# Constants of a recurrent unit computed ahead, and two norms of a token block emitted whole at one stage boundary

## The chip, the cores and the metric

One Trainium2 chip, one core. The metric is the device time of one execution in microseconds (us). TensorE multiplies matrices, VectorE, ScalarE and GpSimd (DVE, ACT and POOL in the rows) work elementwise, and SyncE (SP) issues most DMAs.

## The reference, cut to what matters

512 tokens of width 1024 go through two blocks of a first kind (token mixer, convolutional FFN, each with a residual and a LayerNorm) and then two of a second kind. The first block of the second kind opens with an RMS norm and a gated recurrent unit. The change touches the boundary between the two kinds, and the constants of the recurrent unit:

```python
# end of the last block of the first kind
ffn = conv_ffn(x, ffn_w_up[l], ffn_conv_w[l], ffn_conv_b[l], ffn_w_down[l])
x = layer_norm(ALPHA * x + ffn, ln2_g[l], ln2_b[l])
...
# start of the second kind
hn = rms_norm_2(x, g[0])
proj = x @ w_in + b_in                        # x is hn here
...
log_a = -LRU_C * r_gate * jax.nn.softplus(-lam.astype(jnp.float32))
a = jnp.exp(log_a)
mult = jnp.sqrt(-jnp.expm1(2.0 * log_a))
```

`lam` is a vector of 1024 values that is known at the start. Its softplus does not depend on the tokens.

## The kernel before

Everything is fp32. Each product of two matrices is made of three matmuls of rounded high and low parts (`mm3`, L323 to L325): high by high, low by high, high by low. So the tokens are kept transposed as two tiles, `xTh` (written by ScalarE, L329) and `xTl` (written by VectorE, L331). Weights come in by DMA from SyncE's queue, are rounded on ScalarE (L285) and get their low part on GpSimd (L286).

The 512 tokens are four blocks of 128 rows; `x[:, t, :]` is block t. In the second FFN (`ffn` with `pre` set) the last part of the down projection runs block by block. When a block's second half has arrived (L897), `evac` starts a generator for it, `fin_row(t)`. Its first two parts are the LayerNorm `ln_fin`: mean and variance (L465, L467, L469), two halves centred and scaled by ScalarE and GpSimd (L472, L473), an inverse root by three Newton rounds of one-column VectorE rows (`rs1`, L411 to L417), then the scaling pair (L479; in block 3 also L477). The rest is the RMS norm `pre_norm`: squares with a sum on ScalarE (L944), the product with the gain into `work`, one half on GpSimd and one on VectorE (L960), another inverse root (L949 and `rs1`), and then a diagonal matrix `dg` with the root on it (L964). TensorE multiplies `work` by `dg` (L969), which scales and transposes at once, four 128x128 tiles into each of two banks named `tr`; L329 and L331 take each bank out to `xTh` and `xTl`.

`skew` keeps the open generators in a list. A call with a new generator moves every open one by one part, so consecutive blocks are in different parts; a call without one runs all that are open to their end.

The next stage is `rglru`. It first computes constants from `lam` (`sm8` and `lru` tiles, L1222 to L1242, twenty VectorE rows and one Exp on ScalarE, L1224), then calls `lead`: for its first two weight units it multiplies tokens 0 to 255 and then 256 to 511, 48 matmuls of 128x256 for each half, so that work can begin when two blocks are transposed. Later matmuls are 128x512.

A scheduler with a simulated timeline sets the order of each engine's rows within the dependences, so the order on an engine is not that of the code. A few rows are pinned by hand (`late`, `in_turn`). The activations that need another function table get an `ACT_TABLE_LOAD` in front of them.

Of the kernel before, what the change touches and what calls it, by code (L numbers as in the profile page):

```python
# [197 lines left out]
class Core:  # L198
# [656 lines left out]
    def ffn(self, l, x, xT, pre=None):  # L855

        nc = self.nc
        groups = [range(0, 8), range(8, 16), range(16, 22)]
        hs = {}

        def up(j):
            acc = []
            for o in (0, NF):
                ps = self.tmm(f"wu{l}", o + j, xT)
                a = self.t([128, 512], "tmp", 5, name="fup")
                nc.scalar.activation(a, ps, AF.Identity, scale=self.v(f"fc{l}2", o + j), bias=self.v(f"fb{l}", o + j))  # L866
                for d, tap in ((1, 1), (2, 0)):
                    nc.vector.scalar_tensor_tensor(a[:, d:], ps[:, :512 - d], self.v(f"fc{l}{tap}", o + j), a[:, d:],  # L868
                                                   op0=OP.mult, op1=OP.add)
                acc.append(a)  # L870
            nc.scalar.activation(acc[0], acc[0], AF.Gelu)
            nc.vector.tensor_mul(acc[0], acc[0], acc[1])
            tag = ("q", "k", "pt")[j % 3]
            nb = 9 if tag == "pt" else 8
            hh, hl = self.t([128, S], tag, nb, F32R, "hh"), self.t([128, S], tag, nb, F32R, "hl")
            self.split(hh, hl, acc[0])
            hs[j] = (hh, hl)

        g, b = self.row(4 * l + 2), self.row(4 * l + 3)
        xT2 = self.newT()  # L880
        st = {}
        if pre is not None:
            work = self.workset()

        def down(gi):
            js = list(groups[gi])
            fin = gi == 2
            for cb in range(2):
                nu = len(js) // 2
                u0 = cb * 11 + js[0] // 2  # L890

                def evac(t, ps, cb=cb):
                    s = slice(cb * 512, cb * 512 + 512)
                    if gi == 0:
                        nc.vector.scalar_tensor_tensor(x[:, t, s], x[:, t, s], ALPHA, ps, op0=OP.mult, op1=OP.add)
                    else:
                        nc.vector.tensor_add(x[:, t, s], x[:, t, s], ps)  # L897
                    if fin:
                        self.ln_half(x, t, cb, st)
                        if cb == 1:  # L900
                            self.skew(fin_row(t))
                if fin and cb == 1:
                    self.tokens([hs[j] for j in js], kept, evac)
                    continue
                kept = []

                def keep(i):
                    kept.extend(self.W_in(f"wn{l}", 11 + js[0] // 2 + i, *self.halves(KEEP["ffn"][i])))
                self.nmm(f"wn{l}", u0, [hs[j] for j in js], evac, nk=len(js),
                         side=[lambda i=i: keep(i) for i in range(nu)] if fin else ())  # L910
            if fin:
                self.skew()

        def fin_row(t):
            yield from self.ln_fin(x, t, st, g, b, None if pre is not None else xT2)
            if pre is not None:
                yield from self.pre_norm(x, t, pre, work[t], xT2)

        self.lead(f"wu{l}", LEADS["ffn"], xT)
        for j in range(10):  # L920
            up(j)
        down(0)
        for j in range(10, 18):
            up(j)
        down(1)
        for j in range(18, 22):
            up(j)
        down(2)
        return x, self.pairs(xT2)

# [280 lines left out]
            done = min(g[-1] + 3, 32)  # L1211
            down(gi)

    def rglru(self, x, xT):
        nc = self.nc

        lam = self.v("lam")
        z = self.t([128, 8], "sm8", 8)
        s = self.t([128, 8], "sm8", 8)
        s2 = self.t([128, 8], "sm8", 8)  # L1220
        p = self.t([128, 8], "sm8", 8)
        nc.vector.tensor_scalar(z, lam, -1.0, None, op0=OP.mult)  # L1222
        nc.vector.tensor_max(s, z, lam)
        nc.scalar.activation(s, s, AF.Exp, scale=-1.0)  # L1224
# [7 lines left out]
            nc.vector.scalar_tensor_tensor(p, p, 1.0 / c, s2, op0=OP.add, op1=OP.mult)  # L1232
        nc.vector.scalar_tensor_tensor(p, p, 1.0, s, op0=OP.add, op1=OP.mult)
        nc.vector.tensor_scalar(z, z, 0.0, None, op0=OP.max)
        sp = self.t([128, 8], "lru", 4)
        nc.vector.scalar_tensor_tensor(sp, p, 2.0, z, op0=OP.mult, op1=OP.add)
        m4 = self.t([128, 8], "lru", 4)
        p2 = self.t([128, 8], "lru", 4)
        nc.vector.tensor_scalar(m4, sp, -4.0, None, op0=OP.mult)
        nc.vector.tensor_scalar(p2, sp, 2.0, None, op0=OP.mult)  # L1240
        hb = self.t([128, 16], "lru", 4)
        nc.vector.tensor_scalar(hb, self.v("gb"), 0.5, None, op0=OP.mult)  # L1242
        yT = self.newT()
        self.lead("wli", LEADS["lru"], xT)
        tmp = lambda nm: self.t([128, 512], "tmp", 5, name=nm)
# [629 lines left out]
```

## Time and profile before

| | us |
|---|---|
| runs shown | 3902.67, 3887.15, 3885.52 |
| median | 3887.15 |
| profiled execution, own time | 3890.53 |
| its span on the core | 3888.4 |
| TensorE busy in it | 3684.4 (95%) |
| VectorE, ScalarE, GpSimd busy | 1725.2, 1488.5, 1602.0 |
| mean granted clock of TensorE | 0.969 of full speed |

The span is the time from the core's first to its last recorded instruction; the execution's own time lies 2.1 us above it. Every time in the rows below is counted from the start of that span. A granted clock of 1.00 is the level of 2.4 GHz, 0.50 that of 1.2 GHz.

### The profile page before, as it was taken

Reading aid. Unit: us, or ns where it says so; the run is one execution under the profiler, and the core shown is the slowest. Engines: PE = TensorE matmul, PEld = TensorE weight load, DVE = VectorE, ACT = ScalarE, POOL = GpSimd, SP = SyncE. Lnnn points to the kernel's source line nnn. Section 1 sums busy time; section 2 is a strip of 40 time slices with the busy share of each in tenths; the row PEclk is TensorE's granted clock in tenths of the full one; section 3 lists DMA queues with packets and bytes.
Section 4 is the critical chain, followed back from the end, with each engine's and each line's share of the span. In section 5 each row is a group of like instructions: output and inputs, shape, how many; then the busy total and the mean of one; then the engine's idle time right before and its main releaser. Section 6 shows DMA issues by size and latency. Waiting matters only on the chain.

```text
span 3888.4 us, 54978 instructions
## 1 busy us (share of the span) xinstructions
PE 3684.4 (95%) x21788; PEld 2976.9 (77%) x21788; DVE 1725.2 (44%) x3581; ACT 1488.5 (38%) x2669; POOL 1602.0 (41%) x831
## 2 busy tenths in 40 slices
PE   9999999999999999999998889999898878799998
PEld 8766777888897677778886777888766767688887
DVE  4553254533545424545336754322466564534123
ACT  4433333433344323334333644332364333343322
POOL 4422436444453223444444564344533111443444
PEclk9999999999999999999998999999999868899999
DMA  5311213223342122233331322233323312332332
GB/s 191 117 55 49 89 60 126 92 97 98 111 160 85 55 65 75 79 114 98 98 98 60 103 92 93 82 92 98 109 68 94 75 32 51 125 103 65 95 96 87
DMA packets 158386, 352.96 MB, mean 91 GB/s; under 512 B 63712, under 2 KB 71424, under 8 KB 157872
## 3 DMA queue, kind: packets, MB, share of 16 engines
q1 hardware_dynamic: 157856, 348.61, 28.8%
q8 instruction: 171, 2.80, 0.3%
q0 software_dynamic: 272, 0.84, 0.1%
q14 instruction: 87, 0.71, 0.1%
HBM read 331.53 MB, written 17.86 MB: 90 GB/s over the span
## 4 chain that ended last, share of the span: by engine, by line
PE 77%; DVE 9%; DMA 5%; POOL 4%; ACT 3%; issue 3%; SPq 0%; POOLq 0%; DVEq 0%; ACTq 0%
PE mm L323 13%; PE mm L325 13%; PE mm L324 13%; PE mm L385 6%; PE mm L384 5%; PE mm L386 5%; POOL wlo L286 2%; PE av L384 2%; PE av L386 2%; PE av L385 2%; PE sc L824 2%; PE mm L1687 2%; PE av L653 1%; PE tr L844 1%; ACT whi L285 1%
## 5 line engine op out<-in xcount | busy, mean ns | idle before, releaser
L286 POOL TENSOR_TENSOR wlo<-wst,whi 128x1024 fp32r<-128x1024 f32 (+2 forms) x524 | 1259.1, 2405 | 1789.3 <-PE mm L325 903.6
L285 ACT ACTIVATE whi<-wst 128x1024 fp32r<-128x1024 f32 (+2 forms) x524 | 548.9, 1047 | 1100.3 <-DMA wst<-in_wu 153.1
L323 PE MATMUL mm<-xTh,whi 128*128 128x512 f32 (+1 forms) x2208 | 832.1, 379 | 13.3 <-ACT whi L285 10.3
L324 PE MATMUL mm<-xTl,whi 128*128 128x512 f32 (+1 forms) x2208 | 833.9, 378 | 0.6
L325 PE MATMUL mm<-xTh,wlo 128*128 128x512 f32 (+1 forms) x2208 | 831.7, 378 | 0.0
L323 PEld LDWEIGHTS mm<-xTh,whi 128*128 128x128 f32 x2208 | 415.8, 189 | 100.3 <-ACT whi L285 12.2
L325 PEld LDWEIGHTS mm<-xTh,wlo 128*128 128x128 f32 x2208 | 417.2, 189 | 83.9 <-issue 8.4
L324 PEld LDWEIGHTS mm<-xTl,whi 128*128 128x128 f32 x2208 | 417.4, 189 | 81.3 <-issue 6.8
L868 DVE SCALAR_TENSOR_TENSOR fup<-mm,vec,fup 128x510 f32<-128x510 f32 (+1 forms) x176 | 131.1, 748 | 221.4 <-ACT fup L866 218.5
L830 ACT ACTIVATE P<-sc,sm 128x128 f32<-128x128 f32 x192 | 100.7, 525 | 205.0 <-DVE sm L828 204.7
L827 DVE TENSOR_TENSOR sc<-sc,cst 128x128 f32<-128x128 f32 x192 | 56.2, 297 | 273.4 <-PE sc L826 258.7
L1161 DVE TENSOR_TENSOR relu<-relu,mm 128x512 f32<-128x512 f32 x64 | 43.8, 687 | 295.1 <-ACT relu L1160 295.1
L385 PE MATMUL mm<-wlo,ph 128*128 128x512 f32 x396 | 156.6, 395 | 0.0
L386 PE MATMUL mm<-whi,pl 128*128 128x512 f32 x396 | 154.7, 395 | 0.0
L384 PE MATMUL mm<-whi,ph 128*128 128x512 f32 x396 | 154.5, 396 | 0.0
L385 PE MATMUL mm<-wlo,xTh 128*128 128x512 f32 (+1 forms) x360 | 139.8, 388 | 5.2 <-POOL wlo L286 5.2
L384 PE MATMUL mm<-whi,xTh 128*128 128x512 f32 (+1 forms) x360 | 134.2, 386 | 5.6 <-ACT whi L285 4.8
L386 PE MATMUL mm<-whi,xTl 128*128 128x512 f32 (+1 forms) x360 | 138.6, 386 | 0.0
L1181 DVE TENSOR_TENSOR work<-work,mm 128x512 f32<-128x512 f32 x60 | 41.3, 688 | 170.1 <-PE mm L386 162.2
L969 PE MATMUL tr<-dg,work 128*128 128x128 f32 x384 | 60.5, 324 | 46.6 <-DVE dg L964 20.4
L298 POOL TENSOR_TENSOR wres<-wst,wres 128x512 fp32r<-128x512 f32 (+1 forms) x56 | 83.6, 1508 | 38.5 <-ACT wres L297 33.5
L828 DVE TENSOR_REDUCE sm<-sc 128x1 f32<-128x128 f32 x192 | 93.6, 487 | 4.8
(585 smaller groups left out, 7254.2 us busy)
## 6 DMA issues: line engine op xcount, KB each, us to landing
wst<-in_wu SPq DMA_DIRECT2D x88, 512.0 KB, 3.5
wst<-in_wmu SPq DMA_DIRECT2D x64, 512.0 KB, 3.5
wst<-in_wmd SPq DMA_DIRECT2D x64, 512.0 KB, 3.5
wst<-in_wg SPq DMA_DIRECT2D x48, 512.0 KB, 3.5
wst<-in_wn SPq DMA_DIRECT2D x44, 512.0 KB, 3.5
wst<-in_wa SPq DMA_DIRECT2D x24, 512.0 KB, 3.5
wst<-in_wb SPq DMA_DIRECT2D x24, 512.0 KB, 3.5
wst<-in_wd SPq DMA_DIRECT2D x24, 512.0 KB, 3.5
```

The source lines that it names most:

```text
L285: nc.scalar.activation(hi, st, AF.Copy)
L286: nc.gpsimd.tensor_sub(lo, st, hi.bitcast(F32))
L298: nc.gpsimd.tensor_sub(lo, st[:, s], hi.bitcast(F32))
L323: mm(out, lh, rh, start=start, stop=False)
L324: mm(out, lh, rl, start=False, stop=False)
L325: return mm(out, ll, rh, start=False, stop=stop)
L384: mm(o, xh, hi[:, s], start=k == 0, stop=False)
L385: mm(o, xh, lo[:, s], start=False, stop=False)
L386: mm(o, xl, hi[:, s], start=False, stop=k == nk - 1)
L828: nc.vector.tensor_reduce(mx[:, i:i + 1], sc[:, :n], axis=AX.X, op=OP.max, negate=True)
L830: nc.scalar.activation(P[:, o:o + n], sc[:, :n], AF.Exp, bias=mx[:, i:i + 1], accum_out=rs[:, i:i + 1])
L868: nc.vector.scalar_tensor_tensor(a[:, d:], ps[:, :512 - d], self.v(f"fc{l}{tap}", o + j), a[:, d:], op0=OP.mult, op1=OP.add)
```

## The change

The constants move from `rglru` into a function of their own, `lru_consts`, which the second FFN calls between its tenth up projection and the first part of the down projection; their tiles get tags of their own and the results are kept in `self.lruc`. And behind the `skew` call for a block at the boundary comes a second one without a generator, so all parts of that block are emitted before the next block begins.

```diff
@@ ffn, evac of the down projection
                         if cb == 1:
                             self.skew(fin_row(t))
+                            if pre is not None:
+                                self.skew()
@@ ffn
         for j in range(10):
             up(j)
+        if pre is not None:
+            self.lru_consts()
         down(0)
@@ before rglru
-    def rglru(self, x, xT):
-        nc = self.nc
-
+    def lru_consts(self):
+
+        nc = self.nc
         lam = self.v("lam")
-        z = self.t([128, 8], "sm8", 8)
-        s = self.t([128, 8], "sm8", 8)
-        s2 = self.t([128, 8], "sm8", 8)
-        p = self.t([128, 8], "sm8", 8)
+        z = self.t([128, 8], "lrs", 5)
+        s = self.t([128, 8], "lrs", 5)
+        s2 = self.t([128, 8], "lrs", 5)
+        p = self.t([128, 8], "lrs", 5)
         nc.vector.tensor_scalar(z, lam, -1.0, None, op0=OP.mult)
...
-        sp = self.t([128, 8], "lru", 4)
+        sp = self.t([128, 8], "lrs", 5)
         nc.vector.scalar_tensor_tensor(sp, p, 2.0, z, op0=OP.mult, op1=OP.add)
-        m4 = self.t([128, 8], "lru", 4)
-        p2 = self.t([128, 8], "lru", 4)
+        m4 = self.g([128, 8], "lrm", 2)
+        p2 = self.g([128, 8], "lrm", 2)
         nc.vector.tensor_scalar(m4, sp, -4.0, None, op0=OP.mult)
         nc.vector.tensor_scalar(p2, sp, 2.0, None, op0=OP.mult)
-        hb = self.t([128, 16], "lru", 4)
+        hb = self.g([128, 16], "lrb", 1)
         nc.vector.tensor_scalar(hb, self.v("gb"), 0.5, None, op0=OP.mult)
+        self.lruc = m4, p2, hb
+
+    def rglru(self, x, xT):
+        nc = self.nc
+        m4, p2, hb = self.lruc
         yT = self.newT()
         self.lead("wli", LEADS["lru"], xT)
```

Lines below the first edit move: L949, L960, L964 and L969 of before are L953, L964, L968 and L973 of the changed kernel, L1222 to L1242 are L1226 to L1246, L1292 is L1301; L329, L331 and L411 to L479 stay.

The order of the rows changes most on VectorE at the boundary. Here are the rows of the kernel before up to and with block 0's scale matrix (`dg_16133`); `x_13061` to `x_13064` are blocks 0 to 3, `sm8` tiles belong to the constants.

```order
L479 SCALAR_TENSOR_TENSOR x_13063<-x_13063,rsq_16039,row_13517 128x512 x2
L1226 RECIPROCAL sm8_16247<-sm8_16247 128x8
L416 TENSOR_SCALAR rsq_16063<-rsq_16061,rsq_16062 128x1
L477 SCALAR_TENSOR_TENSOR x_13064<-x_13064,rsq_16094,row_13515 128x512
L411 TENSOR_SCALAR rsq_16100<-rsq_16096 128x1
L413 TENSOR_SCALAR rsq_16101<-rsq_16096 128x1
L960 TENSOR_TENSOR work_13526<-x_13063,row_13513 128x512
L1227 TENSOR_TENSOR sm8_16245<-sm8_16245,sm8_16247 128x8
L417 TENSOR_SCALAR rsq_16061<-rsq_16063,rsq_16061 128x1
...
L1228 TENSOR_TENSOR sm8_16246<-sm8_16245 128x8
L964 TENSOR_SCALAR dg_16133<-cst_66,rsq_16061 128x128
```

In the changed kernel VectorE's rows up to block 0's scale matrix (`dg_16017`) and the ones behind it are these.

```order
L479 SCALAR_TENSOR_TENSOR x_13061<-x_13061,rsq_15984,row_13517 128x512 x2
L465 BN_AGGR bmv_16053<-bst_15930 128x2
L964 TENSOR_TENSOR work_13522<-x_13061,row_13513 128x512
L953 TENSOR_SCALAR rsq_16004<-ss_15997 128x1
...
L417 TENSOR_SCALAR rsq_16006<-rsq_16008,rsq_16006 128x1
L417 TENSOR_SCALAR rsq_16063<-rsq_16065,rsq_16063 128x1
L968 TENSOR_SCALAR dg_16017<-cst_66,rsq_16006 128x128
L416 TENSOR_SCALAR rsq_16065<-rsq_16063,rsq_16064 128x1
L417 TENSOR_SCALAR rsq_16063<-rsq_16065,rsq_16063 128x1
L897 TENSOR_TENSOR x_13064<-x_13064,av_15953 128x512
L479 SCALAR_TENSOR_TENSOR x_13062<-x_13062,rsq_16063,row_13517 128x512 x2
```

Before, 55 rows stood between block 0's L479 pair and its scale matrix, with the scaling of blocks 1 to 3 among them; now it is 22, and block 1's L479 pair stands behind block 0's scale matrix. Block 1's scale matrix follows 26 rows later, block 2's another 24 and block 3's another 15, the last one behind block 2's two L331.

On TensorE the same boundary looked like this before; `work_13521` and `work_13522` are the halves of block 0, then two for each block up to `work_13528`.

```order
L969 MATMUL tr_16135<-dg_16133,work_13521 128x128 x4
L969 MATMUL tr_16142<-dg_16133,work_13522 128x128 x4
L969 MATMUL tr_16174<-dg_16172,work_13523 128x128 x4
L969 MATMUL tr_16181<-dg_16172,work_13524 128x128 x4
L323 MATMUL mm_16287<-xTh_13519,whi_16277 128x256
L323 MATMUL mm_16288<-xTh_13519,whi_16283 128x256
L969 MATMUL tr_16210<-dg_16208,work_13525 128x128 x4
L324 MATMUL mm_16287<-xTl_13520,whi_16277 128x256
```

In the changed kernel TensorE has its rows between block 1's and block 3's transposes in this order.

```order
L973 MATMUL tr_16105<-dg_16096,work_13524 128x128 x4
L323 MATMUL mm_16287<-xTh_13519,whi_16277 128x256
L323 MATMUL mm_16288<-xTh_13519,whi_16283 128x256
...
L324 MATMUL mm_16288<-xTl_13520,whi_16283 128x256
L973 MATMUL tr_16177<-dg_16175,work_13525 128x128 x4
L973 MATMUL tr_16184<-dg_16175,work_13526 128x128 x4
L325 MATMUL mm_16288<-xTh_13519,wlo_16284 128x256
L973 MATMUL tr_16255<-dg_16253,work_13527 128x128 x4
L973 MATMUL tr_16262<-dg_16253,work_13528 128x128 x4
```

Before, the transposes of blocks 2 and 3 were spread among the matmuls of tokens 0 to 255; now 47 of those 48 matmuls stand ahead of block 2's transposes, one between block 2 and block 3, and the other half behind block 3.

VectorE's first rows of the program are these in the changed kernel; `vec_67` is the table of vectors that GpSimd's queue loads, `xTl_79` the low part of the input.

```order
L550 MEMSET KK_718 128x2x17
L1246 TENSOR_SCALAR lrb_14388<-vec_67 128x16
L331 TENSOR_TENSOR xTl_79<-tr_81,xTh_78 128x4x128
L331 TENSOR_TENSOR xTl_79<-tr_88,xTh_78 128x4x128
L331 TENSOR_TENSOR xTl_79<-tr_96,xTh_78 128x4x128
```

The second row is new there: before, it was L1242 at the boundary. The other nineteen rows of the constants now stand at the end of the second mixer, behind the last L479 pair of its LayerNorm and around the L331 of its last block; ScalarE's Exp is there too, with no table load in front of it, and a load appears in front of the first L1301. The number of loads is 19 in both. In the RWKV stage, which the diff does not touch, the scheduler also deals many rows of VectorE, TensorE and ScalarE in another order, above all those of the inverse (L1620, L1622) and of the preparation of units (L1563 to L1585).

## Rows read from the trace of the kernel before

**Rows 1.** The page, busy us, share of the span and instructions.
```profile
PE 3684.4 (95%) x21788; PEld 2976.9 (77%) x21788; DVE 1725.2 (44%) x3581; ACT 1488.5 (38%) x2669; POOL 1602.0 (41%) x831
```
**Rows 2.** Boundary by stretch: length, engines' busy us (instructions), granted clock.
```profile
2090.90:2104.30 13.40, 0.01 (x1) 0.00 (x0) 13.40 (x52) 6.44 (x13) 10.28 (x7) 0.68 0.00 0
2104.30:2111.60 7.30, 3.75 (x16) 3.49 (x16) 7.30 (x35) 2.53 (x6) 1.71 (x1) 0.50 0.00 0
```
**Rows 3.** The same view, a stretch with almost only small VectorE rows.
```profile
2104.13:2106.51 2.38, 2.15 (x10) 2.19 (x11) 2.38 (x22) 0.07 (x1) 0.00 (x0) 0.50 0.00 0
```
**Rows 4.** TensorE's timeline at the boundary: start, length, row, idle time before it.
```profile
2104.36 3.75 PE L969 MATMUL tr<-dg,work 128*128 128x128 f32 x16 [13.44 <-DVE rsq L417]
2111.64 3.75 PE L969 MATMUL tr<-dg,work 128*128 128x128 f32 x16 [3.54 <-DVE dg L964]
...
2130.78 0.28 PE L325 MATMUL mm<-xTh,wlo 128*128 128x256 f32 x1
2130.90 0.40 PE L324 MATMUL mm<-xTl,whi 128*128 128x512 f32 x1
```
**Rows 5.** VectorE's timeline at the boundary.
```profile
2085.07 2.42 DVE L479 SCALAR_TENSOR_TENSOR x<-x,rsq,row 128x512 f32<-128x512 f32 x2 [0.86 <-POOL x L473]
...
2087.54 1.66 DVE L960 TENSOR_TENSOR work<-x,row 128x512 f32<-128x512 f32 x1
...
2103.94 0.27 DVE L964 TENSOR_SCALAR dg<-cst,rsq 128x128 f32<-128x128 f32 x1
...
2116.06 0.69 DVE L331 TENSOR_TENSOR xTl<-tr,xTh 128x512 fp32r<-128x512 f32 x1 [0.19 <-ACT xTh L329]
```
**Rows 6.** VectorE's groups from 2090.9 to 2116.7: busy us, mean ns of one.
```profile
L1229 DVE TENSOR_SCALAR sm<-sm 128x8 f32<-128x8 f32 x1 | 0.2, 152 | 0.0
```
**Rows 7.** Busy time by stretch at the boundary, short stretches.
```profile
2093.00:2096.00 3.00, 0.00 (x0) 0.00 (x0) 3.00 (x7) 1.69 (x5) 3.00 (x2) 0.94 0.00 0
...
2116.00:2117.00 1.00, 1.00 (x10) 1.00 (x9) 0.69 (x1) 0.07 (x2) 0.00 (x0) 0.93 0.03 8
```
**Rows 8.** TensorE's timeline at the end of the second mixer.
```profile
1721.17 1.11 PE L428 MATMUL tr<-cst,x 128*128 128x128 f32 x4 [2.61 <-DVE xTl L331]
...
1726.78 0.40 PE L325 MATMUL mm<-xTh,wlo 128*128 128x256 f32 x1
1726.99 0.30 PE L323 MATMUL mm<-xTh,whi 128*128 128x256 f32 x1
```
**Rows 9.** TensorE's timeline behind the recurrent unit, a block's scaled transposes.
```profile
2295.39 2.02 PE L969 MATMUL tr<-dg,work 128*128 128x128 f32 x16 [0.51 <-DVE rsq L413]
```
**Rows 10.** ScalarE's timeline in the recurrent unit.
```profile
2150.98 0.69 ACT L1282 ACTIVATE gt<-sc,lru 128x512 f32<-128x512 f32 x1 [1.07 <-PE sc L325]
2152.17 1.07 ACT L285 ACTIVATE whi<-wst 128x1024 fp32r<-128x1024 f32 x1 [0.50 <-PE sc L324]
...
2153.82 1.28 ACT L1297 ACT_TABLE_LOAD   x1
2155.12 1.16 ACT L1297 ACTIVATE sq<-sq 128x512 f32<-128x512 f32 x2
```
**Rows 11.** Timelines at the start of the program, and the vector table's load.
```profile
1.26 0.70 POOL L214 DMA_DIRECT2D vec<-in_vec  x1 [0.81 <-POOLq L1867]
...
DMA to landing us min/median/max: 6.4/6.4/6.4
...
6.81 0.69 DVE L331 TENSOR_TENSOR xTl<-tr,xTh 128x512 fp32r<-128x512 f32 x1 [5.90 <-ACT xTh L329]
...
8.67 1.94 PE L428 MATMUL tr<-cst,x 128*128 128x128 f32 x8 [1.67 <-DMA x<-in_x]
```
**Rows 12.** VectorE's timeline at the end of the second mixer.
```profile
1734.10 1.29 DVE L331 TENSOR_TENSOR xTl<-tr,xTh 128x512 fp32r<-128x512 f32 x2 [3.12 <-ACT xTh L329]
```
**Rows 13.** The RWKV stage, 2790 to 3350: TensorE's largest wait group; busy sums.
```profile
PE mm L1687 <- DVE SB L1721: 10.5, 9, 7.2
...
sum 560.00, PE 466.94 PEld 378.48 DVE 328.98 ACT 230.34 POOL 160.23; mean PE 33.35 PEld 27.03 DVE 23.50 ACT 16.45 POOL 11.45
```

## The prediction

> **What bounds the kernel now.** I read the head of the page first [rows 1]: TensorE is busy 3684.4 us, 95% of the span. Time can therefore only be won where TensorE stands still or runs at its lower clock level. So I went to the place that the diff touches, the end of the second FFN, with the table of busy time by stretch [rows 2]. In the first stretch, from the end of the last FFN matmul (2090.9) to 2104.3, TensorE is busy 0.01 of 13.40 us and VectorE 13.40 of 13.40. In the second TensorE does 3.75 of 7.30 us and VectorE again all 7.30. In these 20.7 us VectorE is the bound, and the granted clock is at 0.50 after the first few us. The timeline of TensorE gives the same as events [rows 4]: block 0's scaled transposes start at 2104.36 after 13.44 us of idle that a VectorE instruction ended, block 1's at 2111.64 after 3.54 us, and the leading 128x256 matmuls of the recurrent unit are done at 2130.90. That mark, 2130.9, is the one that I follow below. VectorE's timeline says why block 0 is late [rows 5]: its first norm's last pair (L479) is issued at 2085.07, and its scale matrix (L964) only at 2103.94, 18.9 us later, because the other blocks' work and the constants stand between.
>
> **Step 1, block 0 is emitted whole.** VectorE's new order has 22 rows between block 0's L479 pair and its scale matrix, where there were 55. Three are wide: the work product, which took 1.66 us, and an addition and a statistics row, at about 0.68 us each (the L331 at 2116.06, as wide, took 0.69) [rows 5]. The 19 others are one- or two-column operations; in a stretch that holds almost only these, 22 instructions filled 2.38 us [rows 3], so 0.11 us each. From the pair's end at 2087.5 that is 3.0 + 19 x 0.11 = 5.1 us: scale matrix at 2092.6, not 2103.94. Block 1's comes 26 rows later: an L479 pair (1.4 to 2.42 us), five wide rows (0.6 to 0.68 each, one up to 1.66), and 20 small ones (2.2 us), together 7 to 9 us; I take 8, so 2100.5.
>
> **Step 2, what TensorE makes of it.** Block 1's transposes start at 2100.5, where they started at 2111.64. From their start to the end of the last low half (L331 at 2116.06, 0.69 long) it took 5.1 us at the lower level [rows 4, 5], so the lead can run from 2105.6. TensorE's new order lets 47 of the 48 matmuls of tokens 0 to 255 run there, before the transposes of block 2. A 128x256 matmul starts every 0.12 us at full clock [rows 4] and every 0.21 us at the lower level [rows 8].
>
> When does the clock come back? Before, TensorE was at work without a break from 2111.64, and the clock stood at 0.93 in the us from 2116 [rows 4, 7]: 4.5 us. At the end of the second mixer it worked from 1721.17, and the spacing changed after 1726.99 [rows 8]: 5.8 us. With 5.1 us from 2105.6 it returns at 2110.7: 24 matmuls at 0.21, 23 at 0.12, done at 2113.5. If block 1's transposes already count, it returns near 2105.6, and the 47 take 5.6 us: 2111.2.
>
> Then the tail. A block's transposes take 2.02 us at full clock [rows 9]. Block 3's scale matrix stands on VectorE behind the two low halves of block 2, which are done 1.36 us after block 2's transposes (2116.75 less 2115.39) [rows 4, 5]; with four small rows and the matrix, 0.7 us, that is a new wait of 2.06 us, in which TensorE has one matmul. Block 3's transposes take 2.02, its own low halves 1.36, and 46 matmuls 5.5 us. Sum 2.02 + 2.06 + 2.02 + 1.36 + 5.5 = 13.0 us. End of the lead: 2126.5, or 2124.2 for the early clock, against 2130.9. Gain 4.4 or 6.7; I take **5.0**.
>
> **Step 3, the constants.** Twenty VectorE operations leave this boundary, at 0.15 us for one [rows 6]. Seven of them stood among the 55 rows ahead of block 0's scale matrix and the others behind it; step 1 counts the rows that are left, so they are not credited again. At their new place, the end of the second mixer, they stand behind the last L479 pair. VectorE idles 3.12 us there before the next L331 [rows 12]; about twelve of them ahead of that L331, in a dependent chain with one Exp on ScalarE, need some 2.2 us (13 x 0.15 and a hand-over each way). Cost 0; without that cover the lead's second half would start up to 0.5 us late. The bias half (L1242, now L1246) moves to the program's start and stands ahead of the first L331. It needs the vector table, issued at 1.26 for 0.70 us and landing 6.4 us later [rows 11], so at about 7.7 to 8.4; the first L331 ran at 6.81. Queued behind it are that L331 and then TensorE's next transposes, which wait for a DMA until 8.67 anyway. The cost is 0 to 1.7 us; I take 0.2, since TensorE needs only the first L331's bank back, at about 8.6 to 9.2.
>
> **Step 4, the table load.** The number of loads stays the same (19). The load in front of L1224 goes, where ScalarE had slack, and one appears in front of the recurrent unit's first Exp (L1292, now L1301). A load takes 1.28 us [rows 10]. Behind it ScalarE's rows queue up to two idle times of 1.07 and 0.50 us [rows 10], which take in 1.28; but a weight rounding (L285) stands among them, for which TensorE waits later. So 0 to 1.3 us, and I take 0.3. The Trainium skill, "ScalarE: Activation LUTs", section "What ACT_TABLE_LOAD costs", counts a drain of about 1.38 us beside a load of about 1.28, 2.66 us for a switch; by it the loss here could reach 2.7 us, and the total gain would shrink to about 2. The trace of before agrees with the load alone: the activation after a load at 2153.82 was issued at 2155.12, 1.30 us later [rows 10].
>
> **Step 5, rows that are only dealt anew.** The scheduler's order also changes in the RWKV stage, which the edit doesn't name, above all between VectorE's inverse chain and the unit preparation. TensorE is busy 466.94 of 560 us there, and its largest group of waits on one VectorE line is 10.5 us in 9 waits [rows 13]. Nothing in the rows gives the sign. I take 0 and bounds of 10 us on either side, the size of that group.
>
> **Sum.** -5.0 + 0 + 0.2 + 0.3 + 0 = -4.5 us. The profiled execution took 3890.53 us (2.1 around its span), so 3886.0. The median shown lies 3.4 us below that execution; with the same offset **3882.6 us**.
>
> **Rivals.** (A) The forecast: 3 to 8 us gained at the boundary, little elsewhere, 3879 to 3885. (B) The clock stays low. The first transposes now run early and alone, and TensorE idles on both sides of them. If the clock came back only after the whole lead, 47 matmuls would take 10 us, two blocks' transposes 3.75 each [rows 4], and 46 matmuls 9.8: end 2105.6 + 10 + 3.75 + 2.06 + 3.75 + 1.36 + 9.8 = 2136.3. That is 5.4 us lost, about 3893. It decides from a clock that returns after 2121: then the early start is used up. The clock's fall to 0.94 and then 0.50 some us after the last matmul speaks for it [rows 2, 7]; the two returns after 4.5 and 5.8 us of work speak against it. The Trainium skill, "TensorE: Matmul & The Clock Gate", Part 1, has the throttled state as the default and activity as what releases it; the rows here agree in both directions (0.50 in the idle stretch, 1.00 after work). (C) The slower side: the new order in the RWKV stage leaves the inverse chain later for TensorE, one more group of 10 us, while the boundary gives 5: 3892. It decides from 5 us lost there. Against it: the stage's waits are spread over many lines, and none is over 7.2 us alone. (D) The same re-deal goes the other way, 10 us better: 3872. (E) The edit doesn't move the end: block 0 and block 1 are early, but by step 2 block 3's scale matrix comes only at 2117.6 (2113.5 + 2.02 + 1.36 + 0.7), and if the wait in front of it is 4 us longer than I make it, the end is where it was: 3886 to 3889.
>
> **How the numbers follow.** A 0.50, B 0.16, C 0.13, D 0.12, E 0.09. A alone is 3878 to 3886. The 8-in-10 range must reach into C and D, whose bounds are 10 us, and into B: 3871 to 3895. A change of 0.5% is 19.4 us, about what a measurement can tell from none. No single case reaches it; it takes D or C with a second one of the same sign: faster 0.05, slower 0.03, same 0.92.
>
> **What would show it.** In the changed trace: block 0's scale matrix near 2092.6 after the FFN's last matmul at about 2090.9, block 1's near 2100.5, the clock back near 2111, an idle of about 2 us on TensorE between block 2's and block 3's transposes, the last 128x256 near 2126; a table load of 1.28 us in front of the first L1301; VectorE's first L331 near 8 us. I am wrong if block 0's transposes start early but the lead ends after 2131, if the RWKV stage is more than 5 us longer or shorter, or if TensorE waits after the moved load for more than 1.3 us.

## The result and the profile after

The changed kernel takes 3936.99 us (median of 4 runs, 3932.82 to 3942.92), the kernel before beside it 3886.34 us. The ratio is 1.012 with a 95% interval of 1.0102 to 1.0138: 47 us slower (40 to 54), where 4 us less were forecast and 3895 was the upper end of the range. Here and below, the us of a difference are worked out from the ratio; the two medians differ by 50.7. The profiled execution has a span of 3930.9 us against 3888.4 us.

The first thing to read is the head of the page of the changed kernel, and the groups of the three matmuls of `mm3` (busy us, mean ns):

```profile
PE 3722.3 (95%) x21788; PEld 2977.0 (76%) x21788; DVE 1704.5 (43%) x3581; ACT 1488.9 (38%) x2669; POOL 1606.2 (41%) x831
...
L323 PE MATMUL mm<-xTh,whi 128*128 128x512 f32 (+1 forms) x2208 | 843.7, 384 | 12.1 <-ACT whi L285 10.4
L324 PE MATMUL mm<-xTl,whi 128*128 128x512 f32 (+1 forms) x2208 | 844.4, 383 | 1.0 <-DVE xTl L331 0.4
L325 PE MATMUL mm<-xTh,wlo 128*128 128x512 f32 (+1 forms) x2208 | 842.7, 383 | 0.0
```

The same groups on the page of the kernel before:

```profile
L323 PE MATMUL mm<-xTh,whi 128*128 128x512 f32 (+1 forms) x2208 | 832.1, 379 | 13.3 <-ACT whi L285 10.3
L324 PE MATMUL mm<-xTl,whi 128*128 128x512 f32 (+1 forms) x2208 | 833.9, 378 | 0.6
L325 PE MATMUL mm<-xTh,wlo 128*128 128x512 f32 (+1 forms) x2208 | 831.7, 378 | 0.0
```

TensorE runs the same 21788 instructions, its mean granted clock is 0.969 in both, and yet it is busy 38 us longer [rows 1]. The time in which it is not busy hardly grew, from 204.0 to 208.6 us; each matmul became longer. Since matmuls overlap, their spacing, from the start of one to the start of the next, says it best. TensorE's timeline of the kernel before in a stretch of the first FFN, far ahead of the changed boundary:

```profile
1000.05 0.39 PE L325 MATMUL mm<-xTh,wlo 128*128 128x512 f32 x1
1000.28 0.39 PE L323 MATMUL mm<-xTh,whi 128*128 128x512 f32 x1
...
1003.00 0.39 PE L323 MATMUL mm<-xTh,whi 128*128 128x512 f32 x1
```

The same matmuls in the changed kernel:

```profile
1009.79 0.39 PE L323 MATMUL mm<-xTh,whi 128*128 128x512 f32 x1
1010.02 0.40 PE L324 MATMUL mm<-xTl,whi 128*128 128x512 f32 x1
...
1012.82 0.40 PE L324 MATMUL mm<-xTl,whi 128*128 128x512 f32 x1
```

Thirteen steps take 2.95 us before (227 ns each) and 3.03 us after (233 ns), at full clock, with no wait between them, in code that the diff doesn't touch. The changed kernel is already 11.6 us late there: the matmul that starts at 1009.79 started at 998.24 before. When the last FFN matmul ends it is 21 us late (2112.12 against 2090.91).

What the edit does touch is memory. It allocates `lrm` and `lrb`, 128 bytes per partition, in the lasting pool behind the transposed tokens (`xTh`, `xTl`) and ahead of the weights. In the built program the tokens stay where they were, and the weights and phase tiles lie 128 bytes higher. In a row `mm<-xTh,whi` the first operand is streamed (512 columns) and the second is held (128x128). I took all 128x512 matmuls of the three-part products that follow each other within 215 to 250 ns and sorted their spacing by held less streamed address, modulo 256 bytes (what is left of the difference when multiples of 256 are taken off):

```
distance (bytes)      0              64             128            192
kernel before         8314: 227.7    2222: 233.3      94: 232.7    461: 230.2
changed kernel        1157: 227.6    2220: 233.2    7251: 232.9    458: 229.4
                      (number of matmuls: mean ns from start to start)
```

Some 7157 matmuls went from distance 0 to 128, at 5.2 ns each: 37 us. That became theory A.

The boundary itself did most of what steps 1 and 2 said. TensorE's timeline of the changed kernel:

```profile
2111.73 0.39 PE L318 MATMUL av<-wres,hl 128*128 128x512 f32 x1
2115.36 2.02 PE L973 MATMUL tr<-dg,work 128*128 128x128 f32 x16 [3.25 <-DVE dg L968]
2123.10 3.75 PE L973 MATMUL tr<-dg,work 128*128 128x128 f32 x16 [5.71 <-DVE dg L968]
2133.10 1.95 PE L973 MATMUL tr<-dg,work 128*128 128x128 f32 x16
2138.41 3.75 PE L973 MATMUL tr<-dg,work 128*128 128x128 f32 x16 [3.24 <-DVE dg L968]
2149.07 0.40 PE L324 MATMUL mm<-xTl,whi 128*128 128x512 f32 x1
```

The idle of 13.44 us in front of block 0's transposes is 3.25 [rows 4], and the lead is done 36.95 us after the last FFN matmul (2149.07 less 2112.12), where it took 39.99: 3.0 us gained.

Last, the RWKV stage, between the same two TensorE records in both (the 12951st and the 19601st), as busy time by stretch. Before:

```profile
2830.50:3403.00 572.50, 482.89 (x6652) 392.72 (x6651) 327.47 (x806) 229.45 (x575) 170.14 (x145) 0.87 0.28 75
```

After:

```profile
2854.70:3441.40 586.70, 486.94 (x6651) 392.33 (x6650) 325.19 (x803) 227.40 (x573) 171.72 (x146) 0.86 0.27 74
```

It is 14.2 us longer and TensorE is busy only 4.1 us of them; the other 10 us are waits. Two that stand behind the unit preparation grew by 5.1 us together (waits of TensorE, the kernel before and then the changed one; us in total, times, longest):

```profile
PE mm L1687 <- DVE wse L1724: 6.2, 5, 2.9
PE sc L1583 <- POOL kr L1570: 4.4, 3, 2.6
```

```profile
PE mm L1696 <- DVE wse L1733: 8.1, 13, 2.9
PE sc L1592 <- POOL kr L1579: 7.6, 4, 3.5
```

A wait of 3.4 us for the inverse (L1629, once L1620) is new, and some others shrank. A list by line does not account for all of the 10 us.

### The profile page after: what moved, and what is told of

It reads as the page before. It is cut to its first block, busy times and chain, and to the rows that moved or that the text cites. A ratio compares the mean times of both kernels' runs of the same rounds, so it can differ in the third digit from the quotient of the medians.

```text
span 3930.9 us, 54964 instructions
## 1 busy us (share of the span) xinstructions
PE 3722.3 (95%) x21788; PEld 2977.0 (76%) x21788; DVE 1704.5 (43%) x3581; ACT 1488.9 (38%) x2669; POOL 1606.2 (41%) x831
## 5 line engine op out<-in xcount | busy, mean ns | idle before, releaser
L323 PE MATMUL mm<-xTh,whi 128*128 128x512 f32 (+1 forms) x2208 | 843.7, 384 | 12.1 <-ACT whi L285 10.4
L324 PE MATMUL mm<-xTl,whi 128*128 128x512 f32 (+1 forms) x2208 | 844.4, 383 | 1.0 <-DVE xTl L331 0.4
L325 PE MATMUL mm<-xTh,wlo 128*128 128x512 f32 (+1 forms) x2208 | 842.7, 383 | 0.0
L973 PE MATMUL tr<-dg,work 128*128 128x128 f32 x384 | 58.5, 318 | 43.0 <-DVE dg L968 22.3
```

The costliest lines, as they stand in the source:

```text
L323: mm(out, lh, rh, start=start, stop=False)
L324: mm(out, lh, rl, start=False, stop=False)
L325: return mm(out, ll, rh, start=False, stop=stop)
```

## The experiments

Theory A has three terms: distances in memory (+37 us), the RWKV stage's new order (+9 to +13), the boundary (-3 to -5). Rival B puts the loss on the order of rows alone. The experiments ran on three chips, which took 3894 to 3896 us for the kernel before, so ratios are compared.

**One tile wider, nothing else.** The kernel before, with every tile behind the norms 128 bytes higher:

```diff
-        mv = self.g([128, 2], "bmv", 4)
+        mv = self.g([128, 10], "bmv", 4)[:, 0:2]
```

> Kernel before, no edit of the change; one tile of the norms is made 32 bytes wider in each of its four buffers, so every tile allocated behind it (weights, phase tiles) lies 128 bytes higher per partition, the transposed tokens stay, and the order of all rows is the kernel before's. Theory A (a 128x512 matmul with transposed tokens as one operand and a weight as the other runs slower when their distance in memory changes by 128 bytes): these matmuls go from 227 to about 232.7 ns, about 37 us more, near 3923 us. Rival B (the order of the rows costs the 50 us): no change, near 3886 us.

Measured: 3924.91 us, ratio 1.0085 (1.0072 to 1.0099), 33 us slower. The order of the rows is the kernel before's, so rival B cannot explain any of it. TensorE's timeline of this run:

```profile
1010.99 0.40 PE L325 MATMUL mm<-xTh,wlo 128*128 128x512 f32 x1
...
1014.25 0.40 PE L324 MATMUL mm<-xTl,whi 128*128 128x512 f32 x1
```

Fourteen steps in 3.26 us: 233 ns.

**The changed kernel with its tiles elsewhere.** The lasting constant tiles are allocated ahead of the tokens:

```diff
+        self.lrt = [self.gb.tile([128, n], F32, name=f"lrt{n}{i}") for i, n in enumerate((8, 8, 16))]
         self.ident_r = self.sb.tile([128, 128], F32R, name="ident_r")
...
-        m4 = self.g([128, 8], "lrm", 2)
-        p2 = self.g([128, 8], "lrm", 2)
+        m4, p2, hb = self.lrt
```

> The changed kernel with its three lasting constant tiles allocated ahead of the tokens instead of behind them, so tokens, weights and phase tiles all lie 128 bytes higher and their distances are the kernel before's; the order of the RWKV stage is the changed kernel's. Theory A: spacing back to 227 ns, about 37 us less than the changed kernel; what is left against before is the RWKV stage's new order, about 13 us more, and 3 to 5 us less at the boundary and the mixer: near 3892 to 3896. Rival B: like the changed kernel, 3937. Rival C (the weights' own addresses are bad, whatever the tokens'): 3937 too, since they lie 128 bytes higher here as well.

Measured: 3901.33 us, ratio 1.0026 (1.0013 to 1.0039), 10 us slower instead of 47. The weights lie 128 bytes higher here too, so their own address is not what costs (rival C falls). Its timeline:

```profile
1000.01 0.39 PE L325 MATMUL mm<-xTl,whi 128*128 128x512 f32 x1
...
1003.18 0.39 PE L324 MATMUL mm<-xTh,whi 128*128 128x512 f32 x1
```

Fourteen steps in 3.17 us: 226 ns again. At the boundary:

```profile
2092.47 2.78 PE L974 MATMUL tr<-dg,work 128*128 128x128 f32 x16 [3.42 <-DVE dg L969]
2100.21 3.73 PE L974 MATMUL tr<-dg,work 128*128 128x128 f32 x16 [4.96 <-DVE dg L969]
2110.24 1.95 PE L974 MATMUL tr<-dg,work 128*128 128x128 f32 x16
2115.51 2.02 PE L974 MATMUL tr<-dg,work 128*128 128x128 f32 x16 [3.19 <-DVE dg L969]
2123.67 0.40 PE L325 MATMUL mm<-xTl,whi 128*128 128x512 f32 x1
```

The last FFN matmul ends at 2089.05 here, so the lead takes 34.6 us, 5.4 less than before. Block 3's transposes take 2.02 us where they took 3.75 in the changed kernel; that is most of the difference between 5.4 and 3.0.

**One part of the change at a time.** First the second `skew` call alone, then the constants alone (with the early tiles of the run above).

```diff
                             self.skew(fin_row(t))
+                            if pre is not None:
+                                self.skew()
```

> Kernel before with only the second skew call; no tile moves in memory. Theory A: spacing stays at 227 ns; the boundary gains 2 to 4 us; TensorE's order of the RWKV stage is the changed kernel's, so about 13 us are lost there: near 3896. Rival B: most of the 50 us if the emission order is what costs, 3925 to 3937.

```diff
+        if pre is not None:
+            self.lru_consts()
         down(0)
```

> Kernel before with only the constants moved ahead, their lasting tiles allocated ahead of the tokens, so that no distance changes. Theory A: 227 ns, the boundary within 2 us of before, the RWKV stage's order is nearly that of the run with the second skew call alone, so about 13 us are lost there: near 3899. Rival B: up to 3937 if moving the constants is what costs.

Measured: 3905.86 us, ratio 1.0036 (1.0023 to 1.0048), and 3905.19 us, ratio 1.0029 (1.0019 to 1.0039). Either part alone costs 11 to 14 us. Both get nearly TensorE's new order in the RWKV stage, 700 to 1300 us behind the edit, and both lose it there (the table below). At the boundary the first ends its lead 1.7 us sooner than before and the second 1.0.

**The boundary without the new RWKV order.** The second `skew` only for blocks 0 and 1, early tiles; with that the scheduler gives TensorE and ScalarE the kernel before's order in the RWKV stage.

```diff
-                            if pre is not None:
+                            if pre is not None and t < 2:
```

> The changed kernel with its lasting constant tiles ahead of the tokens (distances as before) and the second skew call for blocks 0 and 1 alone; with that the order of the RWKV stage on TensorE and ScalarE is the kernel before's again. Theory A (three terms: boundary -3 to -5 us, RWKV stage's new order about +9, distances +41): only the boundary's gain is left, so 3 to 6 us less than the kernel before. Rival B (the new order in the RWKV stage costs nothing, and the 10 us left over when distances are restored come from the constants or the skew themselves): about 10 us more than before.

Measured: 3893.06 us, ratio 0.9990 (0.9981 to 0.9998), 4 us faster (1 to 7). Busy time of its RWKV stage, and then of the run with early tiles:

```profile
2836.40:3409.90 573.50, 483.00 (x6652) 392.70 (x6651) 327.45 (x803) 227.14 (x573) 170.22 (x145) 0.87 0.28 75
```

```profile
2828.50:3414.00 585.50, 482.45 (x6651) 389.10 (x6650) 325.62 (x804) 227.29 (x573) 172.76 (x146) 0.87 0.27 74
```

TensorE is busy 483.0 and 482.5 us; in this pair the new order adds 12 us of waits. With the second `skew` call alone a part shows as busy time instead: 491.1 us, at a granted clock of 0.85 in that stage where it is 0.87 here. Rival B for this run falls.

**Distances improved.** A scratch tile 192 bytes wider brings the phase tiles behind it to a multiple of 256 bytes from the weights; once with the edit above, once in the kernel before.

```diff
-        j = self.nb.tile([128, 512], F32, tag="junk", bufs=1, name="junk")
+        j = self.nb.tile([128, 560], F32, tag="junk", bufs=1, name="junk")
```

> As the run with two blocks, and one scratch tile of the norms is 192 bytes wider, so the phase tiles behind it lie a multiple of 256 bytes from the weights. Theory A: the 2232 matmuls with a weight streaming and a phase tile held go from 233.3 to 227.4 ns and 288 of another kind from 229.7 too, 13 to 14 us less than the run with two blocks, 17 to 20 us less than the kernel before. Rival B (only the tokens' tiles matter): as the run with two blocks.

> Kernel before with only the scratch tile 192 bytes wider; the order of all rows is the kernel before's. Theory A: 13 to 14 us less than the kernel before. Rival B: no change.

Measured: 3885.89 us, ratio 0.9980 (0.9969 to 0.9991), and 3884.14 us, ratio 0.9968 (0.9955 to 0.9980). The second, one number in the kernel before, is the fastest of all, 12.5 us below before (8 to 18), where 13 to 14 were expected from the table alone. Its page has the matmuls with a held phase tile at

```profile
L385 PE MATMUL mm<-wlo,ph 128*128 128x512 f32 x396 | 154.0, 389 | 0.0
...
L384 PE MATMUL mm<-whi,ph 128*128 128x512 f32 x396 | 152.0, 390 | 0.0
```

and on the page of before they are longer:

```profile
L385 PE MATMUL mm<-wlo,ph 128*128 128x512 f32 x396 | 156.6, 395 | 0.0
...
L384 PE MATMUL mm<-whi,ph 128*128 128x512 f32 x396 | 154.5, 396 | 0.0
```

The two edits together gained 8 us (4 to 12), not the 17 to 20 expected. In the two profiled executions the spans differ by 11.9 us (3882.7 and, with two blocks alone, 3894.6), but that is one execution of each, and the RWKV stage of the first is 5.5 us longer than that of the second (the table below). Why the gains don't add up in the medians is open.

**Another distance.** Weights and phase tiles 64 bytes higher than the kernel before has them:

```diff
-        st = self.wp.tile([128, w], F32, tag="wst", bufs=2, name="wst")
+        st = self.wp.tile([128, w + 8], F32, tag="wst", bufs=2, name="wst")[:, :w]
```

> Kernel before with the two buffers that weights land in 32 bytes wider each, so weights and phase tiles lie 64 bytes higher and the tokens stay; order as before. Theory A in its form by distance (held operand 64 bytes ahead of the streamed one, modulo 256, costs 233.3 ns, 64 bytes behind 229.7): about 38 to 41 us more than before, spacing near 233 ns for tokens streamed against weights and near 230 ns for weights streamed against tokens. Rival B (what counts is which half of 256 bytes an operand lies in): the tokens in streaming (96) and the weights (160) are in different halves, 233 ns in both directions.

Measured: 3923.30 us, ratio 1.0071 (1.0058 to 1.0084), 28 us slower (23 to 33): the direction, and less than the 38 expected. The profiled execution was the slowest of the five, so its span says little; TensorE is busy 3718.3 us in it, 34 more than in the trace of before. Why the time grew less than the table gives is open. The spacing: 8123 matmuls at distance 64 with 233.3 ns, 1520 at 192 with 229.4, 1064 at 0 with 227.6. Rival B, by halves of 256 bytes, fails on the 229.4.

**Controls.** The kernel before again, and the kernel before with a tile that is allocated and never used, which I took to give a third order.

> Kernel before without an edit, for a trace on this chip: ratio 1.000, and from the scatter of its RWKV stage against the first trace (560 us) a bound for what two executions of one order differ by; theory A needs it to be well below 10 us.

```diff
+        self.gb.tile([128, 8], F32, name="gap")
         self.ident_r = self.sb.tile([128, 128], F32R, name="ident_r")
```

> Kernel before with one tile of 32 bytes allocated ahead of the tokens and never used; no distance between operands changes, no operation is added, but the scheduler deals the rows of the RWKV stage anew (a third order). Theory A (the order of that stage is worth some us by chance): 227 ns spacing everywhere, and a time that differs from before by the RWKV stage alone, between -5 and +15 us. Rival B (the order there is worth nothing): ratio 1.000 within 0.1%.

Measured: ratio 0.9996 (0.9986 to 1.0006) for both. But the trace of the unused tile does not show a third order. VectorE's, ScalarE's and GpSimd's rows are those of the kernel before, row for row, and TensorE's records differ at 26 of 21788 places, as many as between the two traces of the unedited kernel. So this run is a second repeat, with everything behind the new tile 32 bytes higher and no distance changed. Whether other new orders of the RWKV stage would cost time as well was not tried; the orders that the change and its parts get do.

**The changed kernel with good distances.** Early tiles and the wider scratch tile.

> The changed kernel with its lasting constant tiles ahead of the tokens, and the scratch tile 192 bytes wider as in the aligned runs: boundary as changed, RWKV order as changed, no costly distances. Theory A: +10 (RWKV less boundary, as measured without the alignment) -13 = about 3 us less than the kernel before; its RWKV stage 9 to 14 us longer than that of the kernel before on this chip. Rival B (the aligned gain does not add up): as without it, 10 us more.

Measured: 3894.83 us, ratio 0.9998 (0.9987 to 1.0009), where 3 us less were expected. The good distances pay for the RWKV order. Length of that stage in all runs, between the same two TensorE records (us):

```
order of before, distances of before or better:
  before 572.5, again 575.4, unused tile 579.7, two blocks 573.5, two blocks aligned 579.0,
  before aligned 570.6
order of before, 128 or 64 bytes or mixed distances:    577.5, 580.8, 580.0
order of the changed kernel or nearly so:
  changed 586.7, early tiles 585.6, skew alone 585.9, constants alone 589.2, changed aligned 588.8
```

The first group has a mean of 575.1 and a scatter of 9 us, the last a mean of 587.2; they do not overlap, though the scatter is not "well below 10 us", as theory A wanted it. The new order costs some 12 us; with one trace of each kernel and that scatter, the figure is good to a few us.

**A mix of distances.** High weight parts at 0, 32, 64 and 96 bytes, low parts at 128:

```diff
-        hi = self.wp.tile([128, w], F32R, tag="whi", bufs=4, name="whi")
+        hi = self.wp.tile([128, w + 8], F32R, tag="whi", bufs=4, name="whi")[:, :w]
```

> Kernel before with each of the four buffers of high weight parts 32 bytes wider, so these lie 0, 32, 64 and 96 bytes and the low parts 128 bytes further from the tokens; order as before. Theory A: spacing by distance (held less streamed address, modulo 256) 227 at 0, 233 at 64 and 128, 230 at 192, and values at 32, 96, 160 and 224 that no run so far has shown; the whole kernel 25 to 40 us slower. Rival B (half of 256 bytes counts, not the distance): only two levels, by the halves.

A single execution: 3920.57 us, some 25 us above before. Theory A's map fails here: for tokens against weights, the mean over the three matmuls of a product lies between 231 and 232 ns for high parts at 0, 32, 64 and 96 alike. Rival B fails as well, for 0 and 32 lie in different halves. Where the first two matmuls of the three are at distance 0, they take 229.6 and 232.1 ns and not 227.5: they do not save the third, and it slows them. So the distance of a matmul's own two operands describes a sequence of equal ones; what happens between unlike neighbours is open.

## Why the prediction was wrong

The step that failed is **step 3**, as it was put: "Cost 0". It costed the moved operations, and for these it was right. It did not cost the tiles that the edit adds. Their 128 bytes per partition sit between tokens and weights and cost 33 us (28 to 39) when nothing else is changed. The diff shows them (`self.g(..., "lrm", 2)`, `"lrb"`), and no rival named them; all of mine were about order, the clock or waits. The premise ahead of the steps hid it: "Time can therefore only be won where TensorE stands still or runs at its lower clock level" takes the length of a matmul at full clock as given, and the kernel before with one wider tile was 12.5 us faster with the same rows in the same order.

**Step 5** was mis-sized: 0, with bounds of 10 us. It measured some 12, and 14.2 between the two first traces, over the 5 us that were to show me wrong. Rival C had the place and nearly the size, 10 us, at a chance of 0.13. Its mechanism, one more group of 10 us behind the inverse chain, shows only in part: one new wait of 3.4 us for the inverse, while the largest group (for `SB`, 10.5 us) stands at 11.3, and at 11.2 in the second trace of the kernel before. As the step said, nothing in the rows gave the sign. 33 + 12 - 3 = 42 us against 47 measured (40 to 54); the profiled spans differ by 42.5.

**Step 1** was right. Block 0's scale matrix was to come 1.7 us after the last FFN matmul (2092.6 less 2090.9), block 1's 9.6. VectorE's timeline of the changed kernel:

```profile
2113.93 1.29 DVE L968 TENSOR_SCALAR dg<-cst,rsq 128x128 f32<-128x128 f32 x1
...
2122.23 0.72 DVE L968 TENSOR_SCALAR dg<-cst,rsq 128x128 f32<-128x128 f32 x1
```

That is 1.8 and 10.1 us after 2112.12; only the row itself was longer than the 0.27 of before [rows 5].

**Step 2** was right in size, 5.0 us forecast and 5.4 measured in the run with early tiles, 3.0 in the changed kernel. Part of that is luck, since its terms missed on both sides: block 1's transposes came 11.0 us after the last FFN matmul and not 9.6, and the wait in front of block 3's is 3.2 us and not 2.06, but the clock came back sooner than I took. Busy time by stretch of the changed kernel (length; busy us of TensorE, its weight loads, VectorE, ScalarE and GpSimd, with instructions; granted clock):

```profile
2123.10:2128.00 4.90, 4.53 (x21) 4.24 (x22) 4.66 (x10) 2.41 (x6) 2.72 (x2) 0.55 0.01 3
2128.00:2133.00 5.00, 5.00 (x45) 5.00 (x44) 4.86 (x21) 1.03 (x2) 2.19 (x2) 1.00 0.00 0
2133.00:2138.40 5.40, 2.16 (x20) 1.99 (x19) 5.01 (x14) 2.34 (x6) 1.41 (x1) 0.94 0.01 2
2138.40:2149.00 10.60, 10.60 (x65) 10.50 (x66) 1.38 (x2) 2.50 (x5) 1.17 (x1) 0.71 0.01 2
```

It shows 1.00 from 2128, 4.9 us after block 1's transposes began, the earlier of the step's two cases, and then 0.94 and 0.71: it fell once more in the wait for block 3, as rival B feared for the idle times around the first transposes. The Trainium skill, "TensorE: Matmul & The Clock Gate", Part 1, has the throttled state as the default; the second fall agrees with it.

**Step 3** for its operations, at the program's start and at the end of the second mixer (VectorE, the changed kernel):

```profile
7.36 0.18 DVE L1246 TENSOR_SCALAR lrb<-vec 128x16 f32<-128x16 f32 x1 [6.45 <-DMA vec<-in_vec]
7.57 0.69 DVE L331 TENSOR_TENSOR xTl<-tr,xTh 128x512 fp32r<-128x512 f32 x1
```

```profile
1745.89 0.17 DVE L1226 TENSOR_SCALAR lrs<-vec 128x8 f32<-128x8 f32 x1
...
1749.05 0.69 DVE L331 TENSOR_TENSOR xTl<-tr,xTh 128x512 fp32r<-128x512 f32 x1 [0.90 <-ACT xTh L329]
```

The wait for the table is there, and the first L331 is 0.76 us later than in [rows 11]. But TensorE's first transposes also start 0.75 us later in this trace (5.81 against 5.06, when the input landed), and its first weight matmul starts at 13.40, where it was 13.72: nothing was lost, and of the 0.2 us none shows. The constants ran inside the idle of [rows 12] and left 0.90 us of it.

**Step 4** was right to take little. ScalarE's timeline:

```profile
2164.21 1.28 ACT L1301 ACT_TABLE_LOAD   x1
2165.51 0.82 ACT L1301 ACTIVATE a<-gt,lrm 128x512 f32<-128x512 f32 x1
...
2170.64 1.06 ACT L285 ACTIVATE whi<-wst 128x1024 fp32r<-128x1024 f32 x1 [0.16 <-issue]
```

The load takes the place of the two idle times of [rows 10], of which 0.16 us is left, and the next activation is issued 1.30 us after the load, with no idle time in front of either. TensorE's waits for ScalarE's weights and gates in the recurrent unit did not grow. The drain of 1.38 us that the Trainium skill, "ScalarE: Activation LUTs", section "What ACT_TABLE_LOAD costs", adds does not show here: the measurement decides.

## What to carry to other kernels

A new tile moves every tile behind it: compare the addresses of streamed and held operands before and after an edit, as one compares the order of rows, and put small lasting tiles where no distance between matmul operands changes. If TensorE's busy time grows at the same clock with the same instructions, look at the start-to-start spacing in a stretch that the edit doesn't touch. And where a scheduler deals the rows, an edit of 5 us can cost 12 us a thousand us later: compare the length of untouched stages, and take a third order for one only when the trace shows it.

## What the runs showed of the hardware that was not expected

The spacing of back-to-back 128x512 matmuls in fp32r at full clock depends on how far the held operand lies from the streamed one, modulo 256 bytes: 227.4 to 227.7 ns at 0, 233.2 to 233.3 at 64, 232.4 to 232.9 at 128, 229.4 to 230.5 at 192, the same in all kernels in which the neighbours of a matmul have its distance. Equal addresses modulo 256 for nearly all of them were worth 12.5 us in the kernel before (0.9968). Why the distance matters is not shown; other widths and types of matmul were not sorted. In the one kernel in which the distances of neighbours differ, the three matmuls of a product take 231 to 232 ns on average, which the distance of each by itself does not explain.
